# 78 blocks of 32 token slots instead of 83 in a mixture-of-experts pass, and the experts in another order

## The chip, the cores and the metric

The kernel runs on one core of one Trainium2 chip. The metric is the device time of one execution in microseconds (us). Engines are named as in the profile: PE is TensorE's products, PEld its weight loads, DVE VectorE, ACT ScalarE, POOL GpSimd, SP SyncE, which here issues nearly all DMAs.

## What is computed

One decoder layer on 512 tokens of width 1024, in float32: a mixer (a convolution group and eight attention heads), a LayerNorm, a router that picks 4 of 32 experts for each token, the experts, and a second LayerNorm. Cut to the part that the change touches:

```python
logits = x @ router_w + router_b
top_logit, top_idx = lax.top_k(logits, 4)            # of 32 experts
gate = softmax(top_logit)
# for every token t and each of its four experts e, w_gate[e], w_up[e], w_down[e] are 1024 x 1024:
g = min(x[t] @ w_gate[e] + b_gate[e], 7);  u = clip(x[t] @ w_up[e] + b_up[e], -7, 7)
h = (u + 1) * g * sigmoid(1.702 * g)
out[t] += gate * (h @ w_down[e] + b_down[e])
x = layer_norm(2 ** 0.25 * x + out, ln2_g, ln2_b)
```

How many of the 2048 pairs of token and expert fall to an expert depends on the data. With the reference's inputs the counts are, expert 0 first and then falling: 91, 124, 113, 110, 109, 97, 95, 88, 83, 78, 78, 73, 73, 64, 61, 59, 58, 57, 57, 52, 50, 48, 40, 40, 40, 40, 37, 36, 32, 29, 20, 16.

## The kernel before

Up to about 270 us the mixer and the router run, in an order that a planner makes; the change doesn't touch them. Then come the experts.

**Places, blocks, groups, turns.** The kernel ranks the experts by their token count on the chip (expert 0 stays first); an expert's rank is its *place*. A table written into the program, `NBLK` (L31), gives each place a fixed number of *blocks* of 32 token slots, whatever the counts are: 3 for place 0, then 4 for six places, 3 for eight, 2 for fifteen, 1 for two, 83 in all. Tokens past a place's slots are found by `overflow` (L1340) and taken by a loop behind the main pass, `rounds` (L1358), with 128 slots a round; with no such token it runs no round. The order in which the main pass takes the places is a second table, `TURNS` (L35): a digit for each of the 32 *turns* (0 to 31 below), which is the block count of the place taken; among the places of the same count the lower comes first. `plan` (L38) lays the blocks of successive turns side by side into *groups* of four rows (the partitions 0 to 31, 32 to 63 and so on); the first turn has a group to itself, and so has the last.

**Slots of a group.** For each group `slots` (L1031) makes one-hot matrices (DVE), sums them on TensorE to token numbers and gates, and `gather` (L1008) fetches the tokens' rows with one indirect DMA a block from POOL's queue (L1017). This runs two turns ahead of the group's use. `xpose` (L1049) turns the rows into xTg.

**A turn.** `expert` (L1066) works through six pieces of weights, 2 MB each: four with a quarter of the contraction of gate and up (L1078, pieces 0 to 3 of the turn), two with a half of that of down (L1104, L1107). Per block a gate/up piece is 8 products of 512 columns (16 records in the trace, as float32 weights go in twice). After the fourth piece `swiglu` (L1055) turns each block's sums into the hidden rows hT, on DVE and ACT. For down, two blocks that lie in rows 0 and 1 or 2 and 3 of the same group make a *pair* (L1104, 512 columns, and both blocks' hT are read), a block without such a neighbour goes alone (L1107, 256 columns).

**Loads.** The pieces come through a ring of seven places. When a piece has been used, `advance` (L319) lets SP issue the next piece of the stream (L302, L310), up to seven ahead; near the end of the stream, one place of the ring is held for biases and LayerNorm vectors. The stream is 32 x 6 pieces.

**Work between the pieces.** After each piece `tick` does one step of what else is to be done. Mostly that is `combine` (L1125), a group's sum: one step that makes a matrix on DVE, and four with two halves each of a one-hot product (L1135, L1136) added to acc by DVE (L1137). It is queued when all blocks of a group are done. Where no sum is queued, nothing stands between a turn's pieces. The last turn is written out on its own: between its pieces come the last group's sum and the outputs of the second LayerNorm (L1414).

Of the kernel before, what the change touches and what calls it, by code (L numbers as in the profile page):

```python
# [18 lines left out]
T, D, H, E, NE, TOPK = 512, 1024, 8, 64, 32, 4  # L19
# [8 lines left out]
# Experts are taken in an order of falling token count (expert 0 first, whatever its count); the  # L28
# place in that order sets how many blocks of 32 token slots an expert gets in the main pass.
# Tokens beyond an expert's slots are taken by the loop behind it, 128 at a time.  # L30
NBLK = [3] + [4] * 6 + [3] * 8 + [2] * 15 + [1] * 2  # L31


# the blocks of the places, in the order of the main pass: light and heavy ones take turns, as the loads set the pace
TURNS = "32233234223242232424223422343211"  # L35


def plan():  # L38
    """Places in the order that the main pass takes them, each with its rows (group, row)."""
    by = {n: [p for p in range(1, NE) if NBLK[p] == n] for n in (4, 3, 2, 1)}  # L40
    seq = [0] + [by[int(n)].pop(0) for n in TURNS[1:]]
    rows, n = [], 0
    for p in seq:
        if p == seq[-1]:
            n = -(-n // 4) * 4
        rows.append((p, [((n + b) // 4, (n + b) % 4) for b in range(NBLK[p])]))
        n = max(n + NBLK[p], 4)
    return rows, -(-n // 4)


# column ranges of the constant array
# [28 lines left out]
# how many working buffers the mixer has  # L80
# [10 lines left out]
# how many of a channel's taps the tensor engine makes, and GpSimd adds up  # L91
# [23 lines left out]
class Buf:  # L115
    """Space of one kind: taken when the first task that uses it is placed, given back after the last."""
# [5 lines left out]
class Plan:  # L122
    """The order of a long stretch of instructions: tasks with an engine, a rough duration (us) and what they
    read and write are placed one by one where they can start first; of several, the one with the longest
    path behind it (less its group's lag) goes first. Spaces of a kind are given out in program order; of a bank,
    one engine has to be done before another can begin."""
# [58 lines left out]
    def order(self, lags):  # L185
        """[(start, end, task, engine, {space: place})]"""
# [78 lines left out]
def tile_layer(ctx: ExitStack, tc: tile.TileContext, x, positions, w_in, conv_w, conv_b, conv_ln_g,  # L265
# [22 lines left out]
    def piece():  # L288
        """The next place of the ring, when there is room."""
        i = turn.pop(0)  # L290
        turn.append(i)
        count[0] += 1
        return ring[i].rearrange("p (k a) f -> p k (a f)", a=2)

    def expert_loads(tag, e):
        """The six loads of one expert's weights."""
# [22 lines left out]
    def advance(used=1):  # L319
        """Pieces have been used up: start the loads that now have room."""  # L320
        freed[0] += used
        while stream and count[0] - freed[0] < size[0]:
            stream.pop(0)()
# [24 lines left out]
    # ================= mixer =================  # L348
# [24 lines left out]
    def warm(t, n):  # L373
        """Products that nobody reads: the tensor engine's clock is halved after a pause."""
        for _ in range(n):
            P.matmul(t.rearrange("p (a c) -> p a c", a=4), onesb, onesb[:, None, :].to_broadcast([128, 4, 128]), start=True,
                     stop=True)

    class Late:
        """Space that another use has had before."""  # L380
# [9 lines left out]
    # Working space in pieces, for the projections and the attention, then taken anew for the second half. Between the  # L390
    # transposes of x and the residual, x's place holds more keys, queries and values.
# [20 lines left out]
    def copy(n, dst, src, r, w, **kw):  # L412
        """A copy that either of two engines can make."""
        def f(e):
            (S.activation(dst(), src(), AF.Copy) if e == "A" else V.tensor_copy(dst(), src()))  # L415
        return op("AV", (0.05 + n / 1180, 0.07 + n / 960), f, r, w, **kw)

# [103 lines left out]
    last_pass, conv_last, RING = [], {}, dict(gt=0, a=1, k=2, q=3, v=0)  # L521

    def unit(n, c, pairs=False):
        """x @ w for 128 channels, in three float32r passes; two heads' first halves come before their second ones."""
# [28 lines left out]
    def conv(c):  # L553
        """The first taps as products with diagonal matrices, the next summed by GpSimd, the others added to the products."""
# [46 lines left out]
    def sbuf_tt(o, a, b, opr, r, w, **kw):  # L601
        """An operation on two arrays in SBUF, which either of two engines can make."""
# [8 lines left out]
    # the out projection's operands in upper and lower parts  # L611
# [15 lines left out]
    def pair(c):  # L627
        """q, k, v and the attention of one pair of heads."""
# [23 lines left out]
        def head(tt, h):  # L652
# [6 lines left out]
            # s = -(score / 8 + mask), its least value  # L659
# [37 lines left out]
    pws = []  # L697

    def conv_tail():
        pl.group = "tail"  # L700
        def total(v, key):
            """u[:, 0] = v(0) + .. + v(3), then its sum over partitions."""
# [121 lines left out]
    def bias_parts(gu):  # L824
        pl.group = "bias"
        """Gate or up biases in three bf16 parts, (part, expert) on partitions."""
# [54 lines left out]
    for tt in range(TT):  # L881
# [12 lines left out]
        def choose(e, lst=lst, lg=lg, tt=tt):  # L894
            """The four experts of each token."""
# [32 lines left out]
    # expert 0 comes first whatever the counts: its ranks need no order  # L928
# [11 lines left out]
    # what it takes from here to the first gather  # L940
# [3 lines left out]
    # expert 0's gate and up weights  # L944
# [25 lines left out]
    # ================= experts =================  # L970
# [11 lines left out]
    def hot(members, rank):  # L982
        """One-hot of tokens by slot. Members: (place, first row, rows, first block)."""
# [10 lines left out]
    def by_slot(members, oh, auxp, ps, cols):  # L994
        """Columns of aux by slot."""
# [6 lines left out]
    def by_row(used, ss, ps, cols):  # L1002
        """Columns of ss, each row of slots on all four quarters of the partitions."""
# [4 lines left out]
    def gather(st, sv):  # L1008
        """The rows of x1 that the slots name."""
# [21 lines left out]
    def slots(members, rank, auxp, pool=(sl, "sl")):  # L1031
        """One-hot of tokens by slot; then each slot's token and gate, and the gather of the tokens' rows."""
# [33 lines left out]
    def expert(tag, rows, sel, tick, pool=(gd, "gd"), small=lambda: None, keep=False):  # L1066
        """rows: (group state, row). Gate and up, SwiGLU, down; tick() runs between the pieces."""
# [57 lines left out]
    def combine(st):  # L1125
        """acc += one-hot^T y, in steps."""
# [36 lines left out]
    def last_load():  # L1163
        """A place of the ring, held to the end: down biases, the second LayerNorm's scale and shift."""
# [9 lines left out]
    def begin(i):  # L1174
        """The first half of the slots of the groups that place i of the order newly takes."""
# [26 lines left out]
    # the first group, expert 0 alone: its tokens, then the order of the experts, at last its gates  # L1202
# [22 lines left out]
    # counts and the order of the experts  # L1225
# [21 lines left out]
    # (behind the first gather, so that the next weights come after it)  # L1247
# [3 lines left out]
    # the gates: softmax over each token's four, spread over the experts, in three bf16 parts  # L1251
# [22 lines left out]
    def setup():  # L1274
        """Everything permuted into the order of the experts; the next groups."""
# [31 lines left out]
    def add_bias():  # L1307
        """acc += sum over experts of gate * b_down; then the second LayerNorm's vectors on all partitions."""
# [31 lines left out]
    def overflow():  # L1340
        """Tokens past each place's slots: how many rounds of 128, and where each place's rounds start."""
# [7 lines left out]
        # inclusive running sum over places  # L1349
# [8 lines left out]
    def rounds():  # L1358
        """The tokens past the slots."""
# [44 lines left out]
    # ================= second LayerNorm =================  # L1404
    def stats(z):
        """Mean and deviation of rows of z."""
# [7 lines left out]
    def outputs():  # L1414
        """The output without the last expert's sum; then acc's rows of its slots."""
# [29 lines left out]
    def quarter(t, q):  # L1445
        """The columns of quarter q, for the partitions that hold it."""
        return t[q * 32:(q + 1) * 32].rearrange("p (b q c) -> p q b c", b=8, q=4)[:, q]

    def last_rows():
        """The rows of the last expert's tokens, a quarter of the columns in each quarter of the partitions."""  # L1450
# [19 lines left out]
    for i, (p, rows) in enumerate(order):  # L1470
        def tick(c):
            """Work for other groups, between an expert's pieces."""
# [24 lines left out]
    # the last expert: between its pieces come all other sums and the output that they make; then the tokens past  # L1497
    # the slots, if any; at last its own tokens' rows are made anew
# [6 lines left out]
    # an empty slot's row lies outside  # L1505
# [8 lines left out]
    def tick(c):  # L1514
# [8 lines left out]
        if c == 4:  # L1523
            # (the square root's table, before it is waited for)
# [35 lines left out]
```

## Time and profile before

| | |
|---|---|
| timed runs | 1343.4 us median of 3 (1341.96 to 1344.57) |
| span of the profiled execution (no other time of it is given) | 1349.2 us, mean granted TensorE clock 0.981 |
| TensorE's products, weight loads | 1279.9 us, 578.0 us busy |
| VectorE, ScalarE, GpSimd | 680.5, 293.8, 190.6 us busy |
| moved by DMA | 442.7 MB, 328 GB/s over the span |

A busy TensorE is counted from each product's issue to its end, and products overlap, so the share says that the engine had work, not that it ran at its peak. The page cuts the span into 40 slices of 33.7 us; the experts begin in the ninth. Windows are stretches of the span with each engine's busy time, and the GB/s tell whether the loads ran or rested.

### The profile page before, as it was taken

The numbers are of one execution on the slowest core, as the hardware profiler recorded it, in microseconds if no ns is written. First come the engines' busy times: TensorE is split into PE (matmuls) and PEld (weight loads), VectorE is DVE, ScalarE is ACT, GpSimd is POOL, SyncE is SP. The second block draws the span as 40 slices with busy tenths as digits, with TensorE's granted clock in tenths as the row PEclk, the third lists the DMA queues.
The fourth block names the chain that finished last, engine by engine and source line by source line (L and its number), as shares of the span: only waits on it lengthen the run. The fifth ranks groups of instructions, "written<-read, shape, count | busy, mean of one in ns | idle before, by whom it ended". The sixth has DMA issues, their size and how long they took to land. (4 is left out here: it accounts for less than half of the span.)

```text
span 1349.2 us, 27298 instructions
## 1 busy us (share of the span) xinstructions
PE 1279.9 (95%) x11407; PEld 578.0 (43%) x11407; DVE 680.5 (50%) x1605; ACT 293.8 (22%) x588; POOL 190.6 (14%) x163
## 2 busy tenths in 40 slices
PE   8989999799999999999999999999999999999993
PEld 7767757533243344433333233435433333433241
DVE  6999764754343443544354343534443543354364
ACT  5677774211011010111010011111110100111022
POOL 2863110511101110101001101010201020000002
PEclk9999999799999999999999999999999999999996
DMA  9400334799999998999999999999999999978991
GB/s 293 145 1 25 105 128 127 291 338 380 406 409 406 406 405 318 379 408 405 405 387 397 405 406 407 386 389 352 403 407 408 349 396 407 371 274 334 397 403 70
DMA packets 126250, 442.72 MB, mean 328 GB/s; under 512 B 8359, under 2 KB 16695, under 8 KB 126124
## 3 DMA queue, kind: packets, MB, share of 16 engines
q1 hardware_dynamic: 122092, 429.98, 82.6%
q0 software_dynamic: 4032, 10.95, 2.4%
q8 instruction: 92, 1.51, 0.5%
q14 instruction: 34, 0.28, 0.1%
HBM read 436.64 MB, written 4.33 MB: 327 GB/s over the span
## 5 line engine op out<-in xcount | busy, mean ns | idle before, releaser
L1078 PE MATMUL gd<-wt,xTg 128*32 128x512 f32 x4592 | 522.7, 593 | 1.4 <-DVE xTg L1053 1.4
L1078 PEld LDWEIGHTS gd<-wt,xTg 128*32 128x32 f32 x4592 | 151.4, 110 | 300.6 <-issue 286.5
L1017 POOL DMA_INDIRECT xg<-x1d,idx x83 | 79.6, 959 | 913.4 <-DVE tk L1046 871.2
L1137 DVE TENSOR_TENSOR acc<-acc,cb 128x512 f32<-128x512 f32 x168 | 107.1, 678 | 181.1 <-PE cb L1136 180.9
L1104 PE MATMUL gd<-wt,hT 128*32 128x512 f32 x1344 | 172.4, 605 | 15.4 <-DVE hT L1064 11.1
L1060 ACT ACTIVATE sg<-gm 128x256 f32<-128x256 f32 x83 | 34.6, 417 | 624.7 <-DVE gm L1059 590.1
L1123 DVE TENSOR_TENSOR yl<-gd,wh 32x256 fp32r<-32x256 f32 (+1 forms) x172 | 86.3, 502 | 131.9 <-ACT wh L1121 130.1
L1121 ACT ACTIVATE wh<-gd 32x256 fp32r<-32x256 f32 (+1 forms) x172 | 75.8, 441 | 274.2 <-PE gd L1104 164.1
L1107 PE MATMUL gd<-wt,hT 128*32 128x256 f32 x1600 | 100.3, 380 | 2.9 <-issue 1.3
L1104 PEld LDWEIGHTS gd<-wt,hT 128*32 128x32 f32 x1344 | 50.1, 111 | 115.1 <-issue 85.9
L1059 DVE TENSOR_SCALAR gm<-gd 128x256 f32<-128x256 f32 x82 | 32.8, 400 | 118.3 <-PE gd L1078 118.3
L546 PE MATMUL bk<-wt,wh 128*128 128x512 f32 (+1 forms) x352 | 80.8, 377 | 1.5 <-ACT wh L415 0.8
L1135 PE MATMUL cb<-wh,cg 128*128 128x512 f32 (+1 forms) x168 | 75.4, 449 | 2.0 <-DVE cg L1129 2.0
L1107 PEld LDWEIGHTS gd<-wt,hT 128*32 128x32 f32 x1600 | 57.9, 110 | 44.4 <-issue 12.1
L1078 PE MATMUL gd<-wb,xTg 128*32 128x512 f32 x656 | 76.6, 593 | 0.0
L546 PEld LDWEIGHTS bk<-wt,wh 128*128 128x128 f32 x352 | 61.0, 189 | 14.6 <-ACT wh L415 1.3
L584 DVE SCALAR_TENSOR_TENSOR bk<-u,cT,bk 128x512 f32<-128x512 f32 x88 | 66.2, 752 | 1.8
L1136 PE MATMUL cb<-yl,cg 128*128 128x512 f32 (+1 forms) x168 | 66.8, 398 | 0.0
L1135 PEld LDWEIGHTS cb<-wh,cg 128*128 128x128 f32 (+1 forms) x168 | 32.0, 190 | 56.6 <-issue 36.3
L1063 DVE SCALAR_TENSOR_TENSOR um<-um,tk,sg 128x256 f32<-128x256 f32 x83 | 42.1, 508 | 9.5
L546 PE MATMUL bk<-wt,wl 128*128 128x512 f32 (+1 forms) x176 | 41.8, 379 | 2.3 <-DVE wl L537 2.1
L1011 DVE TENSOR_REDUCE tk<-sl 128x4 f32<-128x8 f32 (+2 forms) x21 | 3.5, 166 | 77.3 <-PE sl L1005 77.3
(336 smaller groups left out, 1259.9 us busy)
## 6 DMA issues: line engine op xcount, KB each, us to landing
wt<-in_exp_w_gate_dram SPq DMA_DIRECT2D x112, 1024.0 KB
wt<-in_exp_w_up_dram SPq DMA_DIRECT2D x112, 1024.0 KB
wt<-in_exp_w_down_dram SPq DMA_DIRECT2D x52, 2048.0 KB
wb<-in_exp_w_down_dram SPq DMA_DIRECT2D x12, 2048.0 KB
wb<-in_exp_w_gate_dram SPq DMA_DIRECT2D x16, 1024.0 KB
wb<-in_exp_w_up_dram SPq DMA_DIRECT2D x16, 1024.0 KB
wt<-in_w_in_dram SPq DMA_DIRECT2D x3, 2048.0 KB
acc<-in_x_dram SPq DMA_DIRECT2D x8, 512.0 KB
```

Source lines behind the costliest of these rows:

```text
L546: P.matmul(b.t[:, ts], w.t[:, k], xx[:, k, ts], start=(pas == 0 and k == 0), stop=(pas == 2 and k == KT - 1))
L584: op("V", 0.663, (lambda j: lambda e: V.scalar_tensor_tensor(b.t, u[:, c, j:j + T], cT[:, c, j:j + 1], b.t, op0=OP.mult, op1=OP.add))(j), ...
L1017: G.indirect_dma_start(out=xg[:, r], out_offset=None, in_=x1d[:, :], in_offset=bass.IndirectOffsetOnAxis(ap=idx[:, r:r + 1], axis=0))
L1063: V.scalar_tensor_tensor(um, um, st["tk"][:, 8 + r:9 + r], sg, op0=OP.mult, op1=OP.mult)
L1078: P.matmul(ps[i][q * 32:(q + 1) * 32], st["xT"][:, r, c * 2 + k], w[:, k, :, :, q], start=False, stop=(c == 3 and k == 1))
L1104: P.matmul(d[j * 32:(j + 1) * 32], st["hT"][:, r + j % 2, c * 4 + k], w[:, k, 2 * (j // 2):2 * (j // 2) + 2], **kw)
L1107: P.matmul(d[j * 32:(j + 1) * 32, 0:256], st["hT"][:, r, c * 4 + k], w[:, k, j], **kw)
L1121: S.activation(st["yh"][o], a, AF.Copy)
L1123: V.tensor_tensor(st["yl"][o], a, st["yh"][o].bitcast(F32), OP.subtract)
L1135: P.matmul(ps, cg[0:n, tt * 128:(tt + 1) * 128], st["yh"][0:n, c], start=True, stop=False)
L1136: P.matmul(ps, cg[0:n, tt * 128:(tt + 1) * 128], st["yl"][0:n, c], start=False, stop=True)
L1137: V.tensor_tensor(acc[:, tt, c], acc[:, tt, c], ps, OP.add)
```

## The change

Two tables are written anew, and comments are taken out. Places 6, 13, 14, 28 and 29 get a block less (4 to 3, 3 to 2, 3 to 2, 2 to 1, 2 to 1). The order of the turns is another one. All else follows from the tables: the groups (21 instead of 22), which blocks are pairs, where sums are queued, and the slot counts that `overflow` compares with.

```diff
-NBLK = [3] + [4] * 6 + [3] * 8 + [2] * 15 + [1] * 2
+NBLK = [3] + [4] * 5 + [3] * 7 + [2] * 15 + [1] * 4
...
-TURNS = "32233234223242232424223422343211"
+TURNS = "32222422422242223331324231433211"
```

The same place in TensorE's row shows what follows. Turn 4 had three blocks, one single and one pair; from its third piece on (wt and wb are pieces of weights in the ring, gd the sums, xTg and hT the rows that are multiplied; x8 is one block):

```order
L1078 MATMUL gd<-wt_1979,xTg 32x512 x24
L1078 MATMUL gd<-wb_1986,xTg 32x512 x24
L1107 MATMUL gd<-wt_70,hT 32x256 x16
L1104 MATMUL gd<-wt_70,hT 32x512 x16
L1107 MATMUL gd<-wt_71,hT 32x256 x16
L1104 MATMUL gd<-wt_71,hT 32x512 x16
```

Turn 4 after the change, from the same piece on:

```order
L1078 MATMUL gd<-wt_1979,xTg 32x512 x16
L1078 MATMUL gd<-wb_1986,xTg 32x512 x16
L1104 MATMUL gd<-wt_70,hT 32x512 x16
L1104 MATMUL gd<-wt_71,hT 32x512 x16
```

It is one pair now, and as before no sum stands between the pieces: the first down product follows the last gate/up product at once, and the single block that came first is gone.

Turn 19 had four blocks, and no sum between its pieces. From its third piece on, on TensorE:

```order
L1078 MATMUL gd<-wt_1922,xTg 32x512 x32
L1078 MATMUL gd<-wt_1979,xTg 32x512 x32
L1107 MATMUL gd<-wb_1986,hT 32x256 x16
L1104 MATMUL gd<-wb_1986,hT 32x512 x16
L1107 MATMUL gd<-wb_1986,hT 32x256 x16
```

After the change it has one block, and a group's sum between the pieces (cb is the sum's bank, wh and yl the experts' rows in two parts, cg the one-hot matrix):

```order
L1078 MATMUL gd<-wt_1979,xTg 32x512 x8
L1135 MATMUL cb<-wh,cg 128x512
L1136 MATMUL cb<-yl,cg 128x512
L1135 MATMUL cb<-wh,cg 128x512
L1136 MATMUL cb<-yl,cg 128x512
L1107 MATMUL gd<-wb_1986,hT 32x256 x16
```

A quarter of the gate/up products stands in a piece, and the sum stands between the last of them and down.

## Rows read from the trace of the kernel before

**Rows 1.** The page: busy us (share), then tenths and GB/s in 40 slices.

```profile
PE 1279.9 (95%) x11407; PEld 578.0 (43%) x11407; DVE 680.5 (50%) x1605; ACT 293.8 (22%) x588; POOL 190.6 (14%) x163
PE   8989999799999999999999999999999999999993
DMA  9400334799999998999999999999999999978991
GB/s 293 145 1 25 105 128 127 291 338 380 406 409 406 406 405 318 379 408 405 405 387 397 405 406 407 386 389 352 403 407 408 349 396 407 371 274 334 397 403 70
```

**Rows 2.** Waits of PE, 364.5 to 1245.4 us: us in total, times, longest.

```profile
PE gd L1104 <- DVE hT L1064: 9.0, 10, 1.1
PE gd L1104 <- issue: 2.2, 1, 2.2
PE gd L1107 <- PE gd L1078: 0.7, 1, 0.7
PE gd L1107 <- DVE hT L1064: 0.7, 4, 0.2
```

**Rows 3.** Windows of turns 13, 14, 20, 16, 3, 22, 12, 19, 30.

```profile
core 0: us, PE busy (x) PEld busy (x) DVE busy (x) ACT busy (x) POOL busy (x), PEclk, DMA share, GB/s
705.40:733.80 28.40, 27.33 (x242) 9.09 (x236) 12.99 (x35) 2.02 (x4) 3.79 (x4) 1.00 1.01 385
733.80:760.80 27.00, 23.70 (x222) 6.71 (x218) 9.27 (x31) 2.02 (x4) 3.80 (x4) 0.94 1.03 405
937.00:963.80 26.80, 26.64 (x311) 12.20 (x304) 14.41 (x40) 3.83 (x10) 3.79 (x4) 1.00 0.99 374
798.40:820.80 22.40, 21.46 (x270) 8.49 (x265) 9.18 (x26) 3.81 (x10) 0.00 (x0) 1.00 1.03 409
364.50:401.80 37.30, 37.30 (x357) 15.17 (x353) 15.88 (x36) 3.62 (x7) 0.00 (x0) 1.00 1.03 408
990.50:1023.20 32.70, 31.92 (x331) 10.90 (x327) 12.85 (x35) 4.23 (x11) 0.00 (x0) 1.00 1.03 408
658.30:705.40 47.10, 47.10 (x420) 15.24 (x416) 18.82 (x42) 4.04 (x8) 0.00 (x0) 1.00 1.01 399
894.80:937.00 42.20, 42.20 (x470) 18.75 (x465) 15.88 (x42) 5.85 (x14) 0.00 (x0) 1.00 0.97 382
1278.50:1297.50 19.00, 17.66 (x156) 7.27 (x152) 8.50 (x16) 4.33 (x9) 0.00 (x0) 1.00 1.01 398
```

**Rows 4.** Timeline of PE in turn 2: start, us, group of instructions [idle before].

```profile
354.18 1.02 PE L1104 MATMUL gd<-wt,hT 128*32 128x512 f32 x2 [2.16 <-issue]
356.31 2.56 PE L1104 MATMUL gd<-wt,hT 128*32 128x512 f32 x12 [1.11 <-DVE hT L1064]
```

**Rows 5.** Windows ahead of, at and behind that pause.

```profile
345.00:353.00 8.00, 7.01 (x65) 1.92 (x64) 1.82 (x7) 0.42 (x1) 3.79 (x4) 1.00 1.03 402
353.00:362.00 9.00, 6.71 (x42) 1.77 (x46) 4.05 (x8) 0.42 (x1) 0.00 (x0) 0.81 1.03 405
361.00:371.00 10.00, 10.00 (x104) 3.83 (x100) 1.87 (x3) 1.18 (x2) 0.00 (x0) 1.00 1.03 409
```

**Rows 6.** Windows: turn 3 to the end, turn 8, a stretch of turn 10.

```profile
364.50:1349.20 984.70, 946.37 (x9307) 361.53 (x9299) 430.02 (x1054) 118.91 (x263) 75.91 (x73) 0.98 0.96 376
543.10:569.90 26.80, 26.64 (x307) 12.24 (x303) 13.12 (x32) 3.83 (x10) 3.79 (x4) 1.00 0.98 370
580.00:605.00 25.00, 25.00 (x300) 10.34 (x296) 13.38 (x31) 3.83 (x10) 0.00 (x0) 1.00 1.03 408
```

**Rows 7.** The page: the gathers, one DMA a block.

```profile
L1017 POOL DMA_INDIRECT xg<-x1d,idx x83 | 79.6, 959 | 913.4 <-DVE tk L1046 871.2
```

**Rows 8.** Timeline of PE in turn 30 (one block): last gate/up, first down piece.

```profile
1286.96 1.92 PE L1078 MATMUL gd<-wt,xTg 128*32 128x512 f32 x16
1291.34 1.93 PE L1107 MATMUL gd<-wt,hT 128*32 128x256 f32 x32 [1.34 <-issue]
```

**Rows 9.** Timeline of PE in the last turn: its last three gate/up pieces.

```profile
1307.41 4.90 PE L1078 MATMUL sl<-wt,xTg 128*32 128x512 f32 x44
```

## The prediction

> **What bounds the kernel now.** I read the page first [rows 1]. TensorE is busy for 95% of the span, and from the eighth of the 40 slices on the DMA engines show 9 and some 405 GB/s: two resources look full at once, in the same stage, the 32 turns of the experts. Which one waits for the other is told by the waits [rows 2]: between 364.5 and 1245.4 us (turns 3 to 28) TensorE's idle time ahead of products is 12.6 us, most of it for VectorE's hT (the hidden rows), and no row names a load. The loads, on the other hand, do rest: in the 26.8 us of a light turn behind a heavy one they ran at 370 GB/s, against 408 in a stretch where they never stop [rows 6]. So TensorE sets the pace, and the loads follow, held back by a ring of seven pieces. They follow closely: a turn's six pieces (12.58 MB) take 30.8 us at 408 GB/s, a gathered group (0.52 MB) 1.3 us more. A turn of two blocks takes less than that on TensorE, one of three or four more.
>
> **The stock of loads.** From 364.5 us, where turn 3 begins, to the end 376 GB/s x 984.7 us = 370.2 MB are moved [rows 6]. Less 2.1 MB of output and 8.9 MB of gathers (68 of the 83 [rows 7], 0.131 MB each) that is 359.2 MB or 171.3 pieces of 2.097 MB, so 20.7 of 192 had landed where piece 18 is wanted: 2.7 pieces ahead, 13.9 us. Turns 0 to 2 are the same in both kernels, so the changed one has this stock too.
>
> **What a turn costs on TensorE.** The windows of nine turns [rows 3], each from its first gate/up product to the next turn's, give the price by block count, by whether a group's sum (combine, five steps) is there to be done between the pieces, and by how the blocks lie in their group:
> A: two blocks as a pair, with a sum, 28.4. B: a pair without a sum, 27.0. C: two single blocks, with a sum, 26.8. J: two singles without, 22.4. D: three blocks with, 37.3. E: three without, 32.7. F: four with, 47.1. G: four without, 42.2. H: one block, with a sum, 19.0.
> A sum costs 4.4 to 4.9 us; a block 42.2 / 4 = 10.5. But light turns are dear: B takes 4.6 us more than J. A pair's down products need both blocks' hidden rows, TensorE has nothing else to do, idles 2.16 and 1.11 us [rows 4], and then runs at a granted clock of 0.81 on average over 9 us, full speed for part of it and 1.2 GHz for the rest; before the pause and 8 us later it is 1.00 [rows 5].
> H is the last but one turn, where the second LayerNorm's vectors are spread too. In the middle I price it from its parts: gate/up and biases 4 x 1.92, down 2 x 1.93, a pause of 1.34 [rows 8], a sum 4.9: 17.8. So 17 to 19, I take 18.
>
> **The change, part by part.** (1) *Five blocks less, one group less.* Alone this is 5 x 10.5 + 4.9 = 57.4 us of TensorE, whatever the order. The gathers, one-hots and swiglu that go with them lie beside TensorE and are worth nothing; the loads stay the same 192 pieces.
> (2) *Another order, and more light turns.* Turns 3 to 28 before: 5 A, 1 B, 5 C, 1 J, 4 D, 4 E, 4 F, 2 G. By the prices 142.0 + 27.0 + 134.0 + 22.4 + 149.2 + 130.8 + 188.4 + 84.4 = 878.2 us, where the trace has 880.9, so the prices hold to 0.3%. After: 6 A (turns 3, 6, 9, 11, 13, 14), 4 B (4, 7, 10, 15), 2 C (21, 23), 5 D (16, 18, 24, 27, 28), 2 E (17, 20), 2 F (5, 8), 3 G (12, 22, 26), 2 H (19, 25): 170.4 + 108.0 + 53.6 + 186.5 + 65.4 + 94.2 + 126.6 + 36.0 = 840.7. That is 37.5 us less. Of the 57.4 some 20 go back: three more B and four more pairs in all, and turns of one block that carry a whole sum's fixed cost.
> (3) *The end.* Turns 29 to 31 have 2, 1, 1 blocks in both; turn 29's blocks lie in two groups now, singles instead of a pair, worth A - C = 1.6 us. The bias sums, the last full group's sum and the outputs come between the same pieces as before, and the last group has two rows instead of three, which costs the same products. From the end of the last gate/up piece, 1312.3, there are 36.9 us to the end [rows 9], unchanged.
> Sum: -39.1 us, 1349.2 to 1310.1 in the profiled execution. That execution is 5.8 us (0.4%) longer than the median of the timed runs; I carry the difference over: 1343.4 - 39.1 = 1304.3.
>
> **Does the stock last?** Per turn it changes by TensorE's time less 30.8 (32.1 where a group is gathered), and it can't pass some 25 us (the ring: one piece in use, five there, one on its way). Before turn 3: 13.9; turn 4: 10.2; turn 5: 5.1, the lowest. Then the heavy turns 5, 8 and 12 bring it back, and at turn 19 it is full. Turn 20: 12.2; 21: 12.8; 22: 7.5; 23: 18.9; 24: 13.6; 25: 18.8; 26: 6.0; 29: full; 31: about 12. So it comes down to one piece three times and never quite to nothing. My count of it is good to a quarter of a piece at turn 3 (the GB/s are whole numbers) and worse later, so 0 to 3 us of waits are to be added. I take 2: **1306 us**.
> As a floor: with loads at 408 GB/s throughout, the last gate/up piece lands (368.1 - 4.2) / 0.408 = 892 us after 364.5, at 1256.5, and 1.9 + 36.9 us behind it the kernel would end at 1295. The forecast stands 15 us above: the loads rest less than before, but do not bound the whole.
>
> **The rivals.**
> *A, the loads take over in places.* If the loads need 3% more per turn than I reckon (32.7 instead of 31.7), the stock is gone by turns 5, 22 and 26, and from the last full ring on the lack adds up: 8 turns x 1 us less the 6 us left, and the same before turns 5 and 16; in all 5 to 12 us, 1309 to 1316. For it: the lows above. Against: the price comes from the same stage with the same gathers.
> *B, pauses at the lows also cost the clock.* Each of the three lows would add a pause of some 2 us and, as in B, 4.6 us of slow products: 20 us, 1324. The same in all 14 turns of two blocks or fewer would be 14 x 4.6 = 64, so 1368 and slower; that wants the stock empty in all of them, and heavy turns refill it.
> The Trainium skill (TensorE: Matmul & The Clock Gate, section "HAM oscillation") describes just that: where a weight piece's products take less time than the wait for the next load, the clock falls at each piece. The trace before agrees for pauses behind hT; a pause for a load isn't in it.
> *C, the loads bound it already.* Then the blocks were hidden, and nothing changes: 1343. For it: DMA at 9 in nearly all slices [rows 1]. Against: [rows 2] and the 370 GB/s.
> The Trainium skill (Perfetto Trace Analysis, "Identifying the Most-Contended Engine") points this way: it calls matmul busy time a bad measure, and asks for weight-load time (43% here) and for bandwidth against a peak of 358 GB/s. The trace shows 408, above that peak, and no wait for loads, so I follow the waits.
> *D, slower: the slots don't hold the tokens.* Five places lose a block. The routing worked out from the reference and its inputs gives place 13 exactly 64 tokens for 64 slots, and place 28 32 for 32; all others have room, and in both kernels none is over. One token more in either and a round of the loop behind the pass runs: slots and gather 10, a whole expert's loads 31 with nothing to hide them, 12 of products behind the last load, a sum 5, and the outputs again 37: 95 us, so 1400. Before, no round ran: the gathers are 83, one for each block [rows 7].
>
> **How the numbers follow.** Forecast (1300 to 1309) 0.66, A 0.20, B 0.07, C 0.02, D 0.03; the rest, faster than forecast because a lone block or a pair without a sum is cheaper than its row, 0.02. The range takes in the forecast and A and its rounding, 1299 to 1318. The measurement tells 0.2% (2.7 us) from no change. Faster: the forecast, A and most of B, 0.94. Same: C, 0.02. Slower: D and the worst of B, 0.04.
>
> **What would show it.** Right: a span near 1310; TensorE's waits still without loads, or with 0 to 3 us at turns 5, 22, 26 or 31; 78 gathers; five stretches (turns 2, 4, 7, 10, 15) with the clock near 0.8 where there were two; loads above 400 GB/s in nearly all slices. Wrong: rows "PE <- DMA wt" of 10 us or more (A), more clock falls than five (B), the span's loss spread over waits for loads (C), gathers beyond 78 (D), or turns of one block far from 18 us.

## The result: 1312.2 us, in a rival's range

| | before | after |
|---|---|---|
| timed runs | 1343.8 us median of 4 (1341.96 to 1344.57) | 1312.2 us median of 4 (1310.04 to 1313.74) |
| ratio | | 0.9763 (95%: 0.975 to 0.9777) |
| span of the profiled execution | 1349.2 us | 1310.2 us |

The kernel is 31.6 us faster. 1312 lies in the range, but above the forecast's own 1300 to 1309 and inside the 1309 to 1316 of rival A, the loads. The profiled span is as forecast (1310.2 for 1310.1), and that is partly luck: two errors of over 15 us cancel in it. Two executions among the runs below took far longer than the rest of their kernel (1882 us of before, beside e0 to e3, and 7023 us of f1); they are left out of every median and ratio.

The page of after, the rows that answer to [rows 1, 7]:

```profile
PE 1231.8 (94%) x10578; PEld 562.2 (43%) x10578; DVE 649.0 (50%) x1516; ACT 280.7 (21%) x551; POOL 185.6 (14%) x158
GB/s 286 165 1 1 129 113 141 241 287 389 408 406 406 408 406 406 409 396 406 409 406 408 406 406 405 409 405 408 405 408 408 405 406 406 391 364 356 409 401 71
L1017 POOL DMA_INDIRECT xg<-x1d,idx x78 | 74.7, 957 | 879.5 <-DVE tk L1046 837.0
```

TensorE lost 48 us of busy time. The loads, which were below 400 GB/s in thirteen of before's slices from the eleventh to the thirty-ninth, stay above it from the eleventh to the thirty-fourth but for one. There are 78 gathers, so no further round ran.

Waits of TensorE in after, 362.5 to 1207.8 us (turns 3 to 28), as [rows 2] for before:

```profile
PE gd L1104 <- DVE hT L1064: 11.0, 13, 1.1
PE gd L1107 <- DMA wt<-in_exp_w_down_dram: 4.9, 4, 1.9
PE gd L1078 <- DMA wt<-in_exp_w_up_dram: 4.9, 3, 2.4
PE gd L1078 <- DVE yl L1123: 2.5, 1, 2.5
PE gd L1078 <- DMA wb<-in_exp_w_up_dram: 1.3, 1, 1.3
```

Three rows name weights, 11.1 us together; before had none. The row of yl I count to them too, 13.6 in all: it is the first product of turn 5, and in two other traces of this kernel (e4 and f0 below) that product starts well before this yl is done, so it doesn't need it.

Windows of turns 7 (B), 19 (H), 20 (E), 22 (G), 23 (C), 24 (D) and 25 (H) of after, and from turn 3 to the end; they answer to [rows 3, 6]:

```profile
493.70:517.60 23.90, 22.04 (x219) 6.51 (x215) 7.48 (x19) 2.02 (x4) 3.78 (x4) 1.00 1.03 405
878.10:898.00 19.90, 15.94 (x153) 6.62 (x144) 13.57 (x32) 3.42 (x9) 0.00 (x0) 1.00 1.03 408
898.00:932.70 34.70, 34.33 (x347) 12.63 (x351) 8.99 (x32) 2.43 (x5) 3.77 (x4) 0.95 1.03 406
962.40:1004.50 42.10, 42.10 (x464) 20.64 (x468) 14.30 (x39) 4.39 (x11) 0.00 (x0) 1.00 1.03 409
1004.50:1031.10 26.60, 26.60 (x311) 12.20 (x307) 14.57 (x40) 3.83 (x10) 3.79 (x4) 1.00 1.03 405
1031.10:1068.40 37.30, 37.30 (x372) 13.86 (x368) 18.33 (x43) 4.26 (x11) 3.78 (x4) 1.00 1.03 406
1068.40:1091.10 22.70, 17.69 (x158) 7.30 (x152) 11.54 (x26) 3.10 (x7) 0.00 (x0) 0.92 1.02 407
362.50:1310.20 947.70, 896.99 (x8498) 342.71 (x8490) 400.63 (x975) 105.71 (x226) 74.71 (x72) 0.98 0.99 391
```

Turns C, D and G cost what they cost before, to 0.2 us. Two kinds don't. The pair without a sum takes 23.9 at a granted clock of 1.00, where [rows 3] have 27.0 at 0.94. And turns 19 and 25 (19.9 and 22.7 for a forecast 18) and 20 (34.7 for 32.7) hold waits for weights and, behind them, slow products.

### The profile page after: what moved, and what is told of

The parts are those of the page before. It is cut to its first block, busy times and chain, and to the rows that moved or that the text cites. A ratio compares the mean times of both kernels' runs of the same rounds, so it can differ in the third digit from the quotient of the medians.

```text
span 1310.2 us, 25490 instructions
## 1 busy us (share of the span) xinstructions
PE 1231.8 (94%) x10578; PEld 562.2 (43%) x10578; DVE 649.0 (50%) x1516; ACT 280.7 (21%) x551; POOL 185.6 (14%) x158
## 5 line engine op out<-in xcount | busy, mean ns | idle before, releaser
L1078 PE MATMUL gd<-wt,xTg 128*32 128x512 f32 x4304 | 494.9, 596 | 9.9 <-DMA wt<-in_exp_w_up_dram 4.9
L1078 PEld LDWEIGHTS gd<-wt,xTg 128*32 128x32 f32 x4304 | 146.3, 110 | 287.4 <-issue 273.8
L1104 PE MATMUL gd<-wt,hT 128*32 128x512 f32 x1472 | 184.7, 594 | 16.2 <-DVE hT L1064 13.2
L1123 DVE TENSOR_TENSOR yl<-gd,wh 32x256 fp32r<-32x256 f32 (+1 forms) x140 | 73.8, 527 | 141.7 <-ACT wh L1121 140.4
L1121 ACT ACTIVATE wh<-gd 32x256 fp32r<-32x256 f32 (+1 forms) x140 | 64.7, 462 | 280.0 <-PE gd L1104 201.3
L1104 PEld LDWEIGHTS gd<-wt,hT 128*32 128x32 f32 x1472 | 54.9, 110 | 126.9 <-issue 83.9
L1059 DVE TENSOR_SCALAR gm<-gd 128x256 f32<-128x256 f32 x77 | 30.9, 401 | 107.9 <-PE gd L1078 107.9
L1078 PE MATMUL gd<-wb,xTg 128*32 128x512 f32 x624 | 73.5, 593 | 1.3 <-DMA wb<-in_exp_w_up_dram 1.3
L1135 PE MATMUL cb<-wh,cg 128*128 128x512 f32 (+2 forms) x160 | 72.4, 453 | 2.2 <-DVE cg L1129 2.2
L1107 PE MATMUL gd<-wt,hT 128*32 128x256 f32 x1056 | 68.0, 387 | 6.2 <-DMA wt<-in_exp_w_down_dram 4.9
L1136 PE MATMUL cb<-yl,cg 128*128 128x512 f32 (+2 forms) x160 | 64.4, 402 | 0.0
L1135 PEld LDWEIGHTS cb<-wh,cg 128*128 128x128 f32 (+2 forms) x160 | 30.8, 192 | 57.9 <-issue 40.4
L1107 PEld LDWEIGHTS gd<-wt,hT 128*32 128x32 f32 x1056 | 41.3, 111 | 31.8 <-issue 11.7
L582 POOL TENSOR_TENSOR cv<-cv,acc 128x512 f32<-128x512 f32 x28 | 40.1, 1435 | 8.2 <-ACT acc L579 6.7
```

The costliest lines, as they stand in the source:

```text
L582: op("G", 1.25, (lambda t: lambda e: G.tensor_tensor(cv[:, c], cv[:, c], t.t, OP.add))(t), [t], [k])
L1078: P.matmul(ps[i][q * 32:(q + 1) * 32], st["xT"][:, r, c * 2 + k], w[:, k, :, :, q], start=False, stop=(c == 3 and k == 1))
L1104: P.matmul(d[j * 32:(j + 1) * 32], st["hT"][:, r + j % 2, c * 4 + k], w[:, k, 2 * (j // 2):2 * (j // 2) + 2], **kw)
L1107: P.matmul(d[j * 32:(j + 1) * 32, 0:256], st["hT"][:, r, c * 4 + k], w[:, k, j], **kw)
L1121: S.activation(st["yh"][o], a, AF.Copy)
L1123: V.tensor_tensor(st["yl"][o], a, st["yh"][o].bitcast(F32), OP.subtract)
```

## Where the two errors come from

The first shows in VectorE's row. Timeline of turn 2 of before, where the first block's products end at 350.3 (as the profile reckons ends; gm is the first step of swiglu, L1059, and waits for them):

```profile
349.71 0.94 POOL L1017 DMA_INDIRECT xg<-x1d,idx  x1 [0.30 <-issue]
351.78 0.42 DVE L1059 TENSOR_SCALAR gm<-gd 128x256 f32<-128x256 f32 x1 [6.03 <-PE gd L1078]
```

The same in turn 7 of after, and TensorE's first down products behind it:

```profile
505.97 0.95 POOL L1017 DMA_INDIRECT xg<-x1d,idx  x1 [0.30 <-issue]
506.63 0.42 DVE L1059 TENSOR_SCALAR gm<-gd 128x256 f32<-128x256 f32 x1 [4.61 <-PE gd L1078]
509.03 1.02 PE L1104 MATMUL gd<-wt,hT 128*32 128x512 f32 x2 [0.75 <-PE gd L1078]
511.16 5.36 PE L1104 MATMUL gd<-wt,hT 128*32 128x512 f32 x48 [1.11 <-DVE hT L1064]
```

In before gm starts 1.13 us after POOL's last gather has ended (350.65), and 1.5 us after its products. In after it starts 0.29 us before that gather ends, and 0.07 us after its products (506.56). So TensorE waits 0.75 + 1.11 where before it waited 2.16 + 1.11 [rows 4], and the clock stays at 1.00. I call this the *hold*. It isn't in the program: e4 below is the same kernel, and has it. Nor is it VectorE that is late: the one thing that gm waits for is TensorE's signal (the rows name it, PE gd L1078), and the semaphore records of the traces have that signal at 351.76 in before and at 506.61 in after, gm 0.02 us behind it both times. What is late is the signal of the first block, 1.46 us behind the end of its products where it is 0.05 in after; that of the second block comes 0.05 us behind its own in both.

The second is the load. Windows of after across the wait at the start of turn 20, and across that of turn 25:

```profile
890.00:899.00 9.00, 6.10 (x80) 3.31 (x84) 6.95 (x18) 1.50 (x4) 0.00 (x0) 0.96 1.03 407
898.00:907.00 9.00, 8.95 (x88) 3.46 (x92) 0.96 (x4) 0.00 (x0) 0.00 (x0) 0.81 1.03 409
1081.00:1091.00 10.00, 6.74 (x72) 3.27 (x66) 4.29 (x12) 1.50 (x4) 0.00 (x0) 0.83 1.02 405
```

TensorE waits 2.44 us for turn 20's first up weights, and then works at 0.81 for 9 us: the engine is busy and late, so part of what the loads cost shows in no wait row.

## The experiments

Chips differ for the kernel before (1343.8 us in the result, 1351.9, 1352.5 and 1351.2 on the three chips used here), so each ratio goes against before on the same chip.

**e0: before again.** No edit.

> The kernel before, unchanged, for a second trace. In the changed kernel's profile the time of a run is its span plus 2 us; the trace of before has a span of 1349.2 us, so 1351 us, while its timed runs have a median of 1343.8. Theory: that trace was of an execution some 8 us longer than the usual one, and the two pairs without a sum (turns 2 and 14, 27.0 us there, 23.5 us in the changed kernel's turn 2) are where it lost most of it: a span of 1340 to 1343 and 23.5 us in these turns. Rival: the span is 1349 again and the two turns have 27.0 us; then the difference lies in the program, not in the execution.

Measured: 1352.57 us, ratio 1.0002 (0.9992 to 1.0012); span 1350.8, turns 2 and 14 take 26.9 and 26.8 us. My theory, that the profile of before was an untypical execution, fell: here it is the rule, hold included, and the timed runs agree with it. It was the runs of 1343 that differed.

**e1: the blocks without the new order.**

```diff
-TURNS = "32222422422242223331324231433211"
+TURNS = "32233234223242232424223421232111"
```

> The 78 blocks with the turns of before: the five digits that lose a block are lowered where they stand (turns 25 to 29 become 1, 2, 3, 2, 1). Theory A (TensorE's work and the loads' stock both count): the light turns stand together at the end, the stock runs out from turn 26 on, TensorE waits for loads for some 25 us; 1310 to 1320 us. Theory B (only TensorE's work counts, loads follow): five blocks and a group less give some 50 us, 1288 to 1296 us.

Measured: 1319.85 us, ratio 0.9763 (0.9739 to 0.9786). Waits of TensorE for weights:

```profile
PE gd L1078 <- DMA wt<-in_exp_w_up_dram: 9.9, 8, 2.6
PE sl L1078 <- DMA wt<-in_exp_w_up_dram: 5.3, 3, 3.2
PE gd L1107 <- DMA wt<-in_exp_w_down_dram: 2.1, 1, 2.1
```

17.3 us in these rows, where some 25 were expected, all of it in turns 27 to 31, at the end of eight turns among which none has four blocks. The five blocks alone gain 32 us and run into the loads. After's ratio is the same 0.9763 in the result, but 0.9708 and 0.9731 on two chips where before takes as long as here (e4 and f0 below). By these the new order adds some 4 to 7 us; it isn't shown, as e1 and after didn't run on one chip.

**e2: the new order with the 83 blocks.**

```diff
-TURNS = "32233234223242232424223422343211"
+TURNS = "32223422423242224332324232433211"
```

> 83 blocks in the new order: turns 4, 10, 16, 19 and 25 have one block more than in the changed kernel, all other turns are as in it. Both theories: TensorE has as much to do as before and waits for no load, so within 5 us of before, 1339 to 1347. A rival in which the order itself brings the gain (fewer single blocks, loads that rest less): 1325 or less.

Measured: 1355.36 us, ratio 1.0026 (1.0014 to 1.0038), and no wait for weights. With 83 blocks this order wins nothing; it costs 3 us.

**e3 and e5: a third of the bytes less, in after and in before.**

```diff
+    lean = [p for p, rows in plan()[0][3:]]
...
-                for gu, src in enumerate((exp_w_gate, exp_w_up)):
+                for gu, src in enumerate((exp_w_gate, exp_w_up)[:1 if tag in lean else 2]):
```

> The changed kernel, but from turn 3 on the up weights aren't loaded (what lies in the ring is multiplied instead): gate/up pieces cost half the load, TensorE's work stays. Theory A: the waits for loads (11.1 us in the trace) and the slow clock behind some of them (about 5) go: 1294 to 1299 us, and no wait for a load. Theory B (the waits are taken back elsewhere, because the work behind them had time to spare): 1307 to 1312.

> The kernel before with the same cut as in the half-of-up run: from turn 3 on the up weights aren't loaded. It is the control for that run. Theory A (before the change no load is waited for): no change, a ratio of 0.998 to 1.002. Rival (loads slow TensorE also without a wait that the profile names): 5 us or more are gained, as in the changed kernel.

Measured: e3 1308.29 us, ratio 0.9685 (0.9651 to 0.9718), on the chip of e0 to e2; e5 1351.58, ratio 0.9993 (0.9983 to 1.0003). The loads cost the kernel before nothing: rival C is out. What they cost the changed one e3 doesn't tell: it ran beside no run of after, and its four runs lie in two groups, 1303.9 and 1304.3 at a mean granted clock of 0.978 and 0.979, 1312.3 and 1312.7 at 0.974 and 0.970. Its trace, of the first group, has no wait for weights, but theory A's 1294 to 1299 was not reached. The answer waits for f2.

**e4: after again.** No edit.

> The changed kernel again, beside the kernel before on the same chip. On the chip of the first three experiments the kernel before took 1352 us, on that of the first result 1344, and there the pairs without a sum cost 23.5 us instead of 27. Theory H: the same pause behind a gather shows here in turns 4, 7, 10 and 15 (fourth piece 5.8 us instead of 4.4), and the waits for loads are a little shorter for it; 1315 to 1321 us beside 1352, a ratio of 0.973 to 0.977. Rival: the program decides; then the pairs have 23.5 us here too, and the time is 1310 to 1313 us, a ratio of 0.971 or less.

Measured: 1313.80 us, ratio 0.9708 (0.9692 to 0.9724), 38.7 us less than before; span 1311.6. Waits of TensorE in turns 3 to 28:

```profile
PE gd L1104 <- DVE hT L1064: 11.3, 12, 1.1
PE gd L1104 <- issue: 8.6, 4, 2.2
PE gd L1078 <- DMA wt<-in_exp_w_up_dram: 1.7, 1, 1.7
```

Timeline of its turn 7, and windows of its turns 7 and 19 and of the stretch behind turn 7's pause:

```profile
508.49 0.95 POOL L1017 DMA_INDIRECT xg<-x1d,idx  x1 [0.30 <-issue]
510.56 0.42 DVE L1059 TENSOR_SCALAR gm<-gd 128x256 f32<-128x256 f32 x1 [6.02 <-PE gd L1078]
```

```profile
496.20:522.90 26.70, 23.43 (x222) 6.68 (x218) 7.47 (x19) 2.02 (x4) 3.79 (x4) 0.94 1.03 405
889.90:907.20 17.30, 15.73 (x156) 6.78 (x152) 12.35 (x29) 1.93 (x6) 0.00 (x0) 1.00 1.02 398
513.00:522.00 9.00, 7.89 (x54) 1.93 (x58) 2.97 (x6) 0.42 (x1) 0.00 (x0) 0.81 1.03 406
```

Here the hold is back (gm 1.12 us behind the last gather's end at 509.44), in turns 4, 7, 10 and 15: four pauses of up to 2.2 us, B turns of 27.0, 26.7, 28.2 and 27.0. And the loads are hardly waited for, 1.7 us for 13.6. Same program, and nearly the same time as in the result: what TensorE loses to the hold, it doesn't lose to the loads. So theory H was right in the turns and wrong in the time, which came out below its 1315 to 1321.

**e6: another order for the 78 blocks**, chosen by the prices of [rows 3] and the count of the stock, with one pair that has no sum instead of five.

```diff
-TURNS = "32222422422242223331324231433211"
+TURNS = "32224213341243222342322324232211"
```

> The same 78 blocks in a third order, in which light and heavy turns follow so that the stock of loads seldom runs out before the end (turns of one block at 6 and 11 early, where the stock can be filled again, and a heavy turn behind every two or three light ones). Theory A: most of the waits for loads go and TensorE's work stays, 8 to 15 us less than the changed kernel on the same chip, 1303 to 1309 us here. Theory B (the waits only move): within 3 us of the changed kernel.

Measured: 1302.75 us (1297.09 to 1304.47), ratio 0.9623 (0.9594 to 0.9651): 11 us under after on the same chip, the best of all. (Its turns of one block are 6 and 10.) Turns 3 to 28 take 833.1 where e4 takes 845.0, turns 0 to 2 3.9 more, and from turn 30 to the end it is 66.8 for 70.3. Waits for weights (the sl row is the last turn's, the others are of turn 16 and the start of 17):

```profile
PE sl L1078 <- DMA wt<-in_exp_w_up_dram: 6.1, 3, 3.2
PE gd L1107 <- DMA wt<-in_exp_w_down_dram: 1.9, 2, 1.7
PE gd L1078 <- DMA wt<-in_exp_w_up_dram: 1.3, 1, 1.3
```

The gain is theory A's, the reason isn't: 9.3 us of waits for weights are more than e4's 1.7. By the prices of [rows 3] turns 3 to 28 of this order cost 821.9 us, for 840.7 in after, and all of that is the four pairs without a sum that have become singles (J is 22.4 for B's 27.0). So the gain is in what the turns cost TensorE.

**e7: the gathers a piece earlier, in before**, to see what the pause follows.

```diff
             if c == 0:
                 middle(new)
+                finish(new)
+                new.clear()
             if c == 0 and i == 1:
                 combs.append(overflow())
-            if c == 1:
-                finish(new)
-                new.clear()
```

> The kernel before, with the gather of a group issued after a turn's first piece instead of its second. Theory H (VectorE's gm waits until some 1.1 us after POOL's last gather): in turns 2 and 14 the gathers are over before gm, and the fourth piece takes 4.4 us instead of 5.8, the fifth 5.2 instead of 6.7, about 3 us less each; the first pieces of the twenty gathering turns get longer by 0.5 to 2 us each, since the slots' products wait for VectorE there, so that the whole is 5 to 30 us slower. Rival (the pause is the program's own, whatever POOL does): 5.8 us again in these two turns.

Measured: 1355.0 us in one run (before 1352.5), less of a loss than the 5 to 30 us expected. In turns 2 and 14 the fourth and fifth pieces fall from 5.8 and 6.8 to 4.36 and 5.18 us: the pause follows the gather. In exchange the first piece of all 20 turns with a gather is longer:

```profile
PE sl L1005 <- DVE tk L1041: 9.1, 20, 1.3
```

**f0 to f3: the loads against light turns, two by two.** If the loads take back what light turns save, then removing the pause in after gains nothing, and gains all of it where the loads have slack. All four ran on one chip: f0 is after, f1 has the gathers earlier in turns 4, 7, 10 and 15, f2 has the edit of e3, f3 both.

```diff
-            if c == 1:
+            if c == (0 if i in (4, 7, 10, 15) else 1):
```

> The changed kernel, unchanged, as the base of the next three on the same chip. Both theories: 1312 to 1315 us. Its four turns of a pair without a sum in which a group is gathered (4, 7, 10, 15) tell which kind of execution this is: some 27 us each, a fourth piece near 5.8, and at most 2 us of waits for loads; or some 23.8 each, a fourth piece near 4.4, and some 11 us of waits for loads.

> The changed kernel with the one-hots, sums and gathers of the coming group queued a piece earlier in turns 4, 7, 10 and 15 alone, so that VectorE is free before swiglu and TensorE's pause behind hT goes. That takes some 2 us of TensorE's time from each of these turns (27 to 25, from the same move in the kernel before), 8 us in all, and adds no work and no bytes. Theory (what light turns save the loads take back): the time falls by 0 to 4 us only, and rows of TensorE waiting for weights grow by 4 us or more, behind turns 4, 15, 19, 21 or 25. Rival (the turns' times simply add up): the time falls by 7 to 9 us and the waits for loads stay as they are in the changed kernel on this chip. If this execution has no pause to begin with, neither moves by over 2 us.

> The changed kernel with the up weights not loaded from the fourth turn on (a third fewer bytes in each turn, the products on whatever lies in the ring; the output is not the reference's). What loads cost the changed kernel here: 2 to 5 us where its pauses are there, 10 to 16 where they are not. No wait for weights is to be seen. Base for the next one.

> Both: half of the up weights left out from the fourth turn on, and the gathers a piece earlier in turns 4, 7, 10 and 15. Loads can take nothing back now. Theory and rival both: 7 to 9 us under the kernel with half of the up weights alone. The theory lives if this difference is at least 4 us larger than the one that the same move makes with all loads; the rival if both differences are the same within 2 us.

Measured, medians in us, with before at 1351.22 on this chip:

| | all loads | half of the up weights less |
|---|---|---|
| gathers as they were | f0 1313.43 (ratio 0.9731, 0.9708 to 0.9754) | f2 1304.16 (0.9667, 0.9643 to 0.9691) |
| gathers earlier in four turns | f1 1313.17 (0.9725, 0.97 to 0.9751) | f3 1297.43 (0.9609, 0.9587 to 0.9632) |

The same move gains 0.3 us with all loads and 6.7 without, more than the 4 of difference that the expectation asked for, if just below the 7 to 9 that it had for f3. The rival (times add up) falls. f2's runs lie in two groups, 1301 to 1302 and 1306 to 1308, so the 6.7 is 4.5 or 10 by which of them one takes; the lower one is just what the expectation asked for. f1 has no usable trace, so that its rows of waits have grown, as the theory also says, isn't shown. That the move worked in it is: the mean granted clock of f1's runs is 0.977 to 0.980, that of f0's 0.970 to 0.975. The runs of the result, whose trace has no hold, have 0.977 to 0.980 too, and the time of f1. Turn 4 in f0:

```profile
387.60:414.90 27.30, 24.12 (x221) 6.89 (x217) 7.48 (x19) 2.02 (x4) 3.78 (x4) 0.94 1.03 406
```

in f2:

```profile
389.70:415.10 25.40, 22.29 (x223) 6.64 (x219) 7.47 (x19) 2.01 (x4) 3.78 (x4) 1.00 0.89 326
```

and in f3:

```profile
389.60:414.20 24.60, 22.32 (x222) 6.88 (x218) 7.47 (x19) 2.02 (x4) 3.79 (x4) 1.00 0.94 334
```

The four turns together take 109.6, 105.1 and 100.1 us, so the move is there, 5.0 from f2 to f3, and f3's clock is at 1.00 but for turn 7 (0.93). From f0 to f2 the loads give 9.3 us, where I expected 2 to 5: of the 10.6 between the two spans 6.6 lie in turns 21, 25 and 26, where f0 waits for weights (4.4 by its wait rows, the rest slow products behind them), and 4.5 in these four turns, which are shorter in f2 though its pauses are there. In f2 the clock is at 1.00 in turns 4 and 10 and falls in 7 and 15 (0.88 and 0.93), in f0 it falls in all four; why is open. f0 has both the hold and those 4.4 us, where its expectation had 2 at most.

## Why the prediction was right in its range and wrong in its middle

The ledger of turns 3 to 28, each turn measured as in [rows 3], with the waits for weights and the slow products behind them taken out into a line of their own:

| | forecast | after, in the result | e4 |
|---|---|---|---|
| 6 A | 170.4 | 170.0 | 171.2 |
| 4 B | 108.0 | 95.6 | 108.9 |
| 2 C | 53.6 | 53.6 | 53.8 |
| 5 D | 186.5 | 186.0 | 186.7 |
| 2 E, 2 F, 3 G | 286.2 | 287.8 | 288.4 |
| 2 H | 36.0 | 34.6 | 34.6 |
| loads | 0 to 3 | 17.7 | 1.4 |
| sum | 840.7 to 843.7 | 845.3 | 845.0 |

*The prices* held to 1% in e4 but for H, 17.3 for 18. The -39.1 of the sum is -38.7 there, and -37.8 in f0.

*B, 27.0,* was the price of an execution with the hold. In the result's trace it is absent, 3.1 us a turn; turn 2 shows what a pair costs with no gather beside it, 23.5 in after and in e4. That was a miss of its own: "turns 0 to 2 are the same" holds for the blocks, but the group gathered in turn 2 before is gathered elsewhere now.

*The stock* (the step that failed, in "Does the stock last?"). I counted what had landed when a piece was wanted, less the pieces used, and let it run down to zero. But the piece that is wanted must itself have landed whole: TensorE waits when the count is below one piece, 5.1 us, not below zero. By the prediction's own count turn 5 thus stood at the limit (5.1), 26 just above (6.0), and 0 to 3 us was right only with B at 27.0. The same count with 5.1 as its floor, 23.9 for B and 17.3 for H gives waits of 3.1 us at turn 5, 4.5 at turn 22 and 2.2 at turn 26, 9.8 in all, and 6.5, 5.3 and 5.9, all but at the floor, at turns 16, 20 and 21. In the trace TensorE waits at these five, 5, 16, 20, 22 and 26 (or in the last pieces ahead of them), and not at 21. The 12.4 us that the absent hold gave back were so taken by the loads: 13.6 of waits and some 4 of slow products.

That count is itself off by a piece at both ends. DMA packets by queue (packets, MB, share), from 364.5 us to the end of before, then from 362.3, 418.46 (the end of turn 5's wait) and 1091.05 us (that of turn 26's) to the end of after; q1 holds the weights:

```profile
q1 hardware_dynamic: 92369, 359.46, 93.0%
q8 instruction: 76, 1.25, 0.5%
q1 hardware_dynamic: 92560, 360.20, 96.1%
q1 hardware_dynamic: 87013, 338.57, 96.0%
q1 hardware_dynamic: 18836, 73.14, 85.8%
```

Less 2.10 MB of outputs and 0.14 of biases and vectors, 357.2 MB of weights were still to come in before where the prediction has 359.2: it had taken the loads of instructions for weights, 1.25 MB of them in q8. So 21.7 pieces had landed, not 20.7, and 3.7 lay ahead of TensorE. After has 3.3 at its turn 3, which it reaches 2 us earlier. And where after's five waits end, 1.6 (turn 5) to 2.2 (turn 26) pieces have moved beyond those that were used: some of the next piece has moved before the wanted one is used. From stock to limit that makes 1.1 to 1.7 pieces, 1.7 in the count above and 2.7 in the prediction.

*The carried difference* (1343.4 - 39.1). Before's profiled execution was 5.8 us longer than its timed runs, and I subtracted that from after too. After doesn't have it: 1312.2, 1313.8 and 1313.4 on three chips where before takes 1343.8, 1352.5 and 1351.2. A kernel with slack in its loads shows a gain of TensorE, one without it doesn't (f0 to f3); so I read the whole miss of 6 us. That the before of the first chip ran without the hold is argued from this, not shown: there is no trace of such a run. On the chip of f0 its eleven runs lie in two groups, 1345.5 to 1348.6 at a mean granted clock of 0.981 to 0.985 and 1350.5 to 1352.5 at 0.977 to 0.979, while f0's five lie together, 1311.6 to 1315.1, as that would have it.

*The rivals.* A is what happened, in its time and at the places named (5, 22, 26) and two more: e1 has it in full, f0 to f3 show it by itself. Its condition, loads that need 32.7 us a turn, did not come: by the q1 rows above a turn's six pieces took 31.9 from turn 3 to turn 26, where the forecast has 31.7. The stock was lost to the cheaper B and to the limit above zero. I gave A 0.20, too little. B is there in small: behind two of the five waits the clock fell, to 0.81 and 0.83; behind the 2.51 us at turn 5 it stayed at 1.00. The Trainium skill (TensorE: Matmul & The Clock Gate, section "HAM oscillation") tells of a clock that falls at each piece where the wait for the next load outlasts the piece's products; this trace agrees: the 2.44 us ahead of turn 20 and the 1.95 us in turn 25 follow pieces of one block, 1.93 us of products, and the 2.51 us at turn 5 follow a pair's, 3.6. C is out by e5, D by the 78 gathers.

*What would show it.* Loads above 400 GB/s in nearly all slices, the gathers and a span of 1310 came; five stretches at 0.8 did not in the result (four in e4, without turn 2), and load rows above 10 us were the sign I had written down for A.

## What to carry to other kernels

When a light stretch is fed by loads that rarely rest, count the stock in pieces, from the queue that carries them alone, and take its limit from a wait in a trace, not as zero. Run the count with the cheapest price of each turn as well as with the measured one: what the engine gains below the limit is no gain. A price with a pause in it is a price of that execution; see whether the pause's own cause is in the program. An order in which the dear form of the light turns is rare was worth another 11 us (e6), though it waited for weights more.

## What the runs showed of the hardware

A signal from TensorE to VectorE reached it 1.3 to 1.5 us behind the end of its products while GpSimd's indirect gathers were on their way (turns 2 and 14 of before, the four turns in e4, f0 and f2), 0.9 to 1.2 us behind the last gather's end, and 0.05 us behind its products in after's trace of the result, for the same instructions in the same order; moved away from the gather (e7, f3) the pause is gone. What makes an execution hold or not stays open. A wait of 2.44 us (turn 20), or the hold's 2.2 and 1.1 us, can be followed by 9 us at a mean granted clock of 0.81, between the two levels of 1.2 and 2.4 GHz (0.5 and 1.00), or by none at all: behind the 2.51 us wait of turn 5 the stretch read 1.00:

```profile
418.00:426.00 8.00, 7.54 (x77) 2.98 (x81) 0.92 (x2) 0.00 (x0) 0.00 (x0) 1.00 1.03 409
```
